# Half of the first layer's scales by TensorE, rotary tables moved ahead of the first products, normalization by k-tile

## The chip, the cores and the metric

The kernel runs on one core of a Trainium2 chip. The metric is device time in microseconds: the median of three runs of the program. Beside it stands one execution that was recorded by the hardware profiler; its span goes from the first to the last instruction.

## What is computed

Two layers of a decoder trunk on 256 tokens of 1024 channels, all in 32-bit floats. The part that the change touches is the start: the modulation of layer 0 from the conditioning vector `c`, and the first normalization.

```python
def rms_norm(x, g):
    xf = x.astype(jnp.float32)
    y = xf * lax.rsqrt(jnp.mean(xf * xf, axis=-1, keepdims=True) + NORM_EPS)
    return (y * g.astype(jnp.float32)).astype(x.dtype)
...
    cos_a, sin_a = rope_tables(positions, MLA_ROPE_DIM)
    cos_b, sin_b = rope_tables(positions, MOBA_HEAD_DIM)
    c_act = jax.nn.silu(c)
    for l in range(DEPTH):
        mod = c_act @ w_mod[l] + b_mod[l]
        sh1, sc1, g1, sh2, sc2, g2 = jnp.split(mod, 6, axis=-1)
        h = modulate(rms_norm(x, mix_norm_g[l]), sh1, sc1)
        y = token_mixer(h, cos_a, sin_a, cos_b, sin_b, w_in[l],
...
        x = x + g1[:, None, :] * y
        h = modulate(rms_norm(x, ffn_norm_g[l]), sh2, sc2)
        x = x + g2[:, None, :] * channel_mixer(h, w_up[l], ffn_dw_w[l], ffn_dw_b[l], w_down[l])
```

`modulate` is `h * (1 + scale) + shift`; `sh1` and `sc1` are parts r = 0 and r = 1 of `mod`, each a product of a 1024 vector with a 1024 x 1024 matrix.

## The kernel before, in words

Channels lie on the 128 partitions, in 8 k-tiles, and the 256 tokens along the free dimension. Each weight tile comes from memory as floats (`raw`, 512 KB for 1024 columns), ScalarE rounds it to `whi` (L211), VectorE takes the rest `wlo` (L213), and TensorE forms three products for each pair (L288, L289, L291). Activations are split likewise into `hh` (ScalarE, L765) and `hl` (VectorE, L766). SP issues all transfers; a semaphore of each of eight transfers is used again by the ninth after it, so an issue waits until the transfer eight places earlier has landed. Every engine works through its instructions in a fixed order, which a scheduler has set when the program was built: an instruction that waits holds all that stand behind it on its engine.

The start of layer 0 goes like this. SP loads the column of `c` (L341), x in four quarters (L343), then the first weight rows. ScalarE squares the eight k-tiles of x (L517), VectorE adds them up (L521), TensorE sums over channels with a column of ones (L525), VectorE scales (L469), GpSimd raises to the power of -1/2 (L470), TensorE spreads the result over the partitions (L499), ScalarE copies it out as `bcs` (L681), and VectorE multiplies all eight k-tiles of x by it (`xn`, in tile `mq`, L683).

The scales and shifts of layer 0 are made by VectorE: for each k-tile `prepare_tile(k)` loads one row tile of the transposed `w_mod` for the shift and one for the scale (`wload_row`, L687), multiplies each by the activated `c` and sums along the row (L692, 128 x 1024), adds the bias (L694) and makes the gain (L697). ScalarE applies gain and shift (L764), then L765 and L766 split the result, and `latents(k)` and `conv_in(k)` issue the first products of that k-tile. This loop over k runs at L758; `prepare_tile(k + 1)` stands between the two. Behind the loop stand the rotary tables: `make_trig` (some twenty VectorE instructions in a dependent chain, L416 to L438, and a sine by ScalarE, L439, which needs another function table), `make_bases` and `make_tables` (L449 to L461). After that come `GLU0` to `GLU3` (L830 with a Tanh, L831), which free the four PSUM banks of `conv_in`, and the first query, key and value products.

Other parts of `mod` are made by `mod_part`: TensorE multiplies the weight columns by `cact` as a stationary block of 32 columns at four column positions (L388), ScalarE copies the sum, TensorE transposes it and VectorE adds the bias.

PSUM has five banks of tag `psa` and three of `psb`.

Of the kernel before, what the change touches and what calls it, by code (L numbers as in the profile page):

```python
# [9 lines left out]
F32 = mybir.dt.float32  # L10
# [3 lines left out]
AF = mybir.ActivationFunctionType  # L14
# [3 lines left out]
P = 128  # L18
S = 256
NB = 2  # L20
D = 1024
# [127 lines left out]
def trunk_kernel(ctx, tc, xT, crow, ccol, pos, invf, modb_d, cols_d, grow_d, wmr, wm, win1, wqkv,  # L149
# [11 lines left out]
    def nm(s):  # L161
        uid[0] += 1
        return f"{s}_{uid[0]}"
# [10 lines left out]
    def mq(n=D):  # L174
        return wk.tile([P, D + 128], F32, tag="mq", name=nm("mq"), bufs=3, align_bytes=LINE)[:, 0:n]
# [11 lines left out]
    def small(n, tag="sm", bufs=12):  # L187
        return wk.tile([P, n], F32, tag=tag, name=nm(tag), bufs=bufs)
# [150 lines left out]
    x = per.tile([P, KD, S], F32, name="x")  # L339
    modb = per.tile([P, L, 48], F32, name="modb")  # L340
    sy.dma_start(cc, ccol)  # L341
    for i in range(4):
        sy.dma_start(x[:, 2 * i:2 * i + 2, :], xT[:, 2 * i:2 * i + 2, :])  # L343

    def load_rest():
        for dst, src in ((modb, modb_d), (posi, pos), (invt, invf)):
            sy.dma_start(dst, src)
        load_cols(0)
    col, grow = {}, {}

# [8 lines left out]
    def cv(l, name):  # L359
        a, b = COLS[name]  # L360
        return col[l][:, a:b]
# [4 lines left out]
    def wload_row(l, r, k, tag=None):  # L366
        return wload(wmr[ROWS.index((l, r)), k], tag or SPARE[(2 * k + r) % 4], 2 if tag else 1)
# [11 lines left out]
    def mod_part(l, r, spare=True):  # L379
# [15 lines left out]
        for q in range(2):  # L395
# [2 lines left out]
        ve.tensor_tensor(mod[l][:, r * 8:r * 8 + 8].rearrange("p (c q) -> p c q", c=4), view,  # L398
                         modb[:, l, r * 8:r * 8 + 8].rearrange("p (c q) -> p c q", c=4),
                         op=ALU.add)  # L400
        yield

    def mod_parts(*parts):
# [266 lines left out]
    def layer(l):  # L670
# [3 lines left out]
        hh, hl = new_h()  # L674
        if l == 0:

            bc = first_stats(crow0[1])
            xn = [mq().rearrange("p (k t) -> p k t", k=4) for _ in range(2)]

            bcs = e1()  # L680
            ac.activation(bcs, bc, AF.Copy)  # L681
            for k in range(KD):
                (gp if XNP and k else ve).tensor_tensor(xn[k // 4][:, k % 4, :], x[:, k, :], bcs, op=ALU.mult)  # L683
            mods0, gains = [], []

            def prepare_tile(k):
                raws0 = [wload_row(0, r, k) for r in range(2)]  # L687
                if k == 0:
                    load_rest()
                accs = small(2, "m0", 4)  # L690
                for r in range(2):
                    ve.scalar_tensor_tensor(raws0[r], raws0[r], 1.0, crow0[0], op0=ALU.mult, op1=ALU.mult,  # L692
                                            accum_out=accs[:, r:r + 1])
                mods0.append(ve.tensor_tensor(mod[0][:, 0:16].rearrange("p (r k) -> p k r", r=2)[:, k, :], accs,  # L694
                                              modb[:, 0, 0:16].rearrange("p (r k) -> p k r", r=2)[:, k, :], op=ALU.add))
                g = small(1, "gs", 12)
                i = ve.scalar_tensor_tensor(g, mod[0][:, 8 + k:9 + k], 1.0, cv(l, "mix_g")[:, k:k + 1],  # L697
                                            op0=ALU.add, op1=ALU.mult)
                gains.append(g)
                if HOLD:  # L700
                    hold[0] = i.ins

            prepare_tile(0)
        else:
            bc = norm_stats(fill)
# [52 lines left out]
        for k in range(KD):  # L758
# [10 lines left out]
            latents(k)  # L769
            if k + 1 < KD:  # L770
                prepare_tile(k + 1)
            else:
                with tc.issue_after(mods0[-1].ins):
                    make_trig()
            conv_in(k)
            if k in C0K:
                gate_c(0, C0K[k], 3, psa)
# [3 lines left out]
        mods = mod_parts(*((*p, False) for p in PARTS[l]))  # L781

        if l == 0:
            make_bases()
            with tc.issue_after(mods0[-1].ins):
                prepare(0)
        ta, tb, cw, gk, hg = prepared[l]


# [528 lines left out]
```

## Time and profile before

| what | us |
|---|---|
| median of 3 runs | 956.33 |
| the three runs | 953.44, 956.33, 961.74 |
| the profiled execution's own time | 960.24 |
| its span | 958.4 |
| TensorE busy | 910.8 |
| VectorE busy | 792.0 |
| ScalarE busy | 553.7 |
| GpSimd busy | 81.9 |

The span is what the rows below are measured in; the profiled execution's own time is 1.84 us longer than its span. Matmuls are pipelined, so busy time of TensorE is not time at its peak rate: the same product can take twice as long in another stretch.

### The profile page before, as it was taken

How to read it: one execution, taken by the hardware profiler on the slowest of the kernel's cores; microseconds unless marked ns; L12 is line 12 of the kernel's file. 1: busy time of each engine (PE TensorE's matmuls, PEld its weight loads, DVE VectorE, ACT ScalarE, POOL GpSimd, SP SyncE). 2: the span in 40 equal slices, each digit the busy share in tenths (PEclk: the TensorE clock that was granted, in tenths of full speed). 3: DMA queues.
4: the chain of work that ended last, by engine and by line, in shares of the span. 5: the costliest groups of instructions: out<-in, count | busy, mean ns of one | idle time of the engine just before them, and what ended most of it. 6: DMA issues, size and time to landing. Idle time of an engine off the chain costs nothing.

```text
span 958.4 us, 18539 instructions
## 1 busy us (share of the span) xinstructions
PE 910.8 (95%) x7262; PEld 852.6 (89%) x7262; DVE 792.0 (83%) x1524; ACT 553.7 (58%) x978; POOL 81.9 (9%) x48
## 2 busy tenths in 40 slices
PE   3999899799999999999899999979999999999998
PEld 2998788798997999999879987769999899999998
DVE  5999799799997899998874999967677798777774
ACT  4577488634655555555643675847565566555551
POOL 1011621300000000000000042231000000000000
PEclk9999999999998999999979999979999999999999
DMA  7966434388896878888753665505557767656641
GB/s 255 388 218 216 140 111 138 125 271 303 289 323 227 287 252 287 294 309 265 227 184 103 193 221 186 176 23 176 189 167 229 264 210 219 185 190 181 193 134 44
DMA packets 58120, 201.07 MB, mean 210 GB/s; under 512 B 6960, under 2 KB 8496, under 8 KB 58032
## 3 DMA queue, kind: packets, MB, share of 16 engines
q1 hardware_dynamic: 58032, 199.88, 62.4%
q8 instruction: 57, 0.93, 0.4%
q14 instruction: 31, 0.25, 0.1%
HBM read 198.81 MB, written 1.05 MB: 209 GB/s over the span
## 4 chain that ended last, share of the span: by engine, by line
PE 68%; DVE 11%; issue 8%; DMA 5%; POOL 4%; ACT 3%; SPq 0%; POOLq 0%; DVEq 0%; ACTq 0%
PE psb L288 13%; PE psb L291 13%; PE psb L289 13%; PE psa L288 6%; PE psa L289 6%; PE psa L291 6%; DVE wlo L213 3%; POOL rs L470 2%; DVE cacc L1015 2%; PE psa L388 2%; DMA raw<-in_wmr 2%; POOL ri L610 2%; ACT p L604 2%; DVE raw L371 1%; PE psa L628 1%
## 5 line engine op out<-in xcount | busy, mean ns | idle before, releaser
L211 ACT ACTIVATE whi<-raw 128x1024 fp32r<-128x1024 f32 (+2 forms) x286 | 294.4, 1037 | 217.0 <-PE psb L289 100.4
L213 DVE TENSOR_TENSOR wlo<-raw,whi 128x1024 fp32r<-128x1024 f32 (+2 forms) x286 | 340.4, 1194 | 82.6 <-ACT whi L211 71.4
L288 PE MATMUL psb<-hh,whi 128*128 128x256 f32 x1088 | 263.6, 283 | 1.2 <-ACT p L604 0.8
L289 PE MATMUL psb<-hl,whi 128*128 128x256 f32 x1088 | 260.8, 280 | 0.0
L288 PEld LDWEIGHTS psb<-hh,whi 128*128 128x128 f32 x1088 | 205.3, 189 | 9.1 <-issue 4.9
L289 PEld LDWEIGHTS psb<-hl,whi 128*128 128x128 f32 x1088 | 205.1, 189 | 1.4 <-DVE hl L534 1.1
L291 PE MATMUL psb<-hh,wlo 128*128 128x256 f32 x1088 | 150.5, 280 | 0.0
L291 PEld LDWEIGHTS psb<-hh,wlo 128*128 128x128 f32 x1088 | 136.8, 189 | 0.9 <-issue 0.8
L1015 DVE SCALAR_TENSOR_TENSOR cacc<-upad,cw,cacc 128x256 f32<-128x256 f32 x240 | 105.0, 480 | 0.4
L470 POOL TENSOR_TENSOR rs<-rs,mhalf 128x16 f32<-128x16 f32 (+3 forms) x22 | 48.8, 2228 | 585.6 <-DVE rs L469 581.5
L288 PE MATMUL psa<-mhl,whi 128*128 128x256 f32 x400 | 95.2, 279 | 0.0
L289 PE MATMUL psa<-mhl,whi 128*128 128x256 f32 x400 | 95.0, 279 | 0.0
L1194 DVE SCALAR_TENSOR_TENSOR e<-psb,fw,e 128x255 f32<-128x255 f32 (+1 forms) x176 | 83.9, 478 | 10.9 <-ACT e L1192 9.7
L288 PEld LDWEIGHTS psa<-mhl,whi 128*128 128x128 f32 x400 | 75.2, 189 | 0.2 <-ACT mhl L1096 0.2
L289 PEld LDWEIGHTS psa<-mhl,whi 128*128 128x128 f32 x400 | 75.2, 188 | 0.0
L1192 ACT ACTIVATE e<-psb,fb,fw 128x256 f32<-128x256 f32 x88 | 48.6, 553 | 34.9 <-DVE e L1194 21.1
L291 PE MATMUL psa<-mhl,wlo 128*128 128x256 f32 x400 | 54.6, 279 | 0.0
L371 DVE SCALAR_TENSOR_TENSOR raw<-raw,crow 128x1024 f32<-128x1024 f32 x40 | 48.7, 1218 | 2.9 <-DMA raw<-in_wmr 2.9
L291 PEld LDWEIGHTS psa<-mhl,wlo 128*128 128x128 f32 x400 | 50.1, 189 | 0.0
L610 POOL TENSOR_TENSOR ri<-smx,minus 128x4 f32<-128x4 f32 x16 | 31.5, 1978 | 93.2 <-ACT p L604 93.2
L288 PE MATMUL psb<-whi,hh 128*128 128x416 f32 (+1 forms) x96 | 32.0, 355 | 7.6 <-ACT hh L765 7.6
L388 PE MATMUL psa<-raw,cact 128*32 128x256 f32 x320 | 32.7, 445 | 0.4 <-DMA raw<-in_wm 0.4
(267 smaller groups left out, 1509.7 us busy)
## 6 DMA issues: line engine op xcount, KB each, us to landing
raw<-in_wup SPq DMA_DIRECT2D x88, 512.0 KB, 4.7
raw<-in_wmr SPq DMA_DIRECT2D x56, 512.0 KB, 5.2
raw<-in_wdn SPq DMA_DIRECT2D x44, 512.0 KB, 4.2
raw<-in_wm SPq DMA_DIRECT2D x40, 512.0 KB, 4.4
raw<-in_wgab SPq DMA_DIRECT2D x32, 512.0 KB, 4.7
raw<-in_wqkv SPq DMA_DIRECT2D x24, 512.0 KB, 4.8
raw<-in_win SPq DMA_DIRECT2D x16, 512.0 KB, 4.8
raw<-in_wgc SPq DMA_DIRECT2D x16, 512.0 KB, 4.2
```

The costliest lines, as they stand in the source:

```text
L211: ac.activation(hi, raw, AF.Copy)
L213: ve.tensor_tensor(lo, raw, hi.bitcast(F32), op=ALU.subtract)
L288: te.matmul(o, p1[0], p1[1], start=start, stop=False)
L289: te.matmul(o, p2[0], p2[1], start=False, stop=False)
L291: te.matmul(o, p3[0], p3[1], start=False, stop=stop)
L371: ve.scalar_tensor_tensor(raw, raw, scale, row, op0=ALU.mult, op1=ALU.mult, accum_out=acc)
L388: te.matmul(acc[32 * c:32 * c + 32, 0:S], cact[:, k:k + 1].to_broadcast([P, 32]), raw[:, c * S:(c + 1) * S], start=(k == 0), stop=(k == KD ...
L470: gp.tensor_tensor(r, r, mhalf[:, :n], op=ALU.pow)
L610: gp.tensor_tensor(ri, sm, minus1[:, 0:4], op=ALU.pow)
L1015: ve.scalar_tensor_tensor(aj, upad[:, j, t:t + S], cw[:, j * 31 + t:j * 31 + t + 1], aj, op0=ALU.mult, op1=ALU.add)
L1192: ac.activation(t, src, AF.Identity, scale=fw[:, 2, c:c + 1], bias=fb[:, c:c + 1])
L1194: ve.scalar_tensor_tensor(t[:, d:S], src[:, 0:S - d], fw[:, 2 - d, c:c + 1], t[:, d:S], op0=ALU.mult, op1=ALU.add)
```

## The change

- A new function `mod_first(0, 1)` makes half of layer 0's scales (r = 1, the channels of k-tiles 0 to 3) on TensorE. It loads the first 512 columns of the untransposed `w_mod` part, all eight k, as four transfers of 512 KB; multiplies them by `cact` in 32 products of 128 columns; copies the sum by ScalarE, transposes it by TensorE, adds the bias by VectorE. One `mod_gain` makes the four gains. `prepare_tile(k)` then has one row instead of two for k < 4.
- The positions and inverse frequencies are loaded before x. `load_rest` (bias, columns, rows of gains) is called behind the four new transfers.
- `make_trig` and `make_bases` are called behind `first_stats`, before the rest of `mod_first`, and no longer behind the loop; `prepare(0)` loses its place behind the last row.
- The multiplication of x by `bcs` moves into `prepare_tile(k)`, one k-tile at a time.

```diff
--- before.py
+++ after.py
@@ -339,12 +339,13 @@
     x = per.tile([P, KD, S], F32, name="x")
     modb = per.tile([P, L, 48], F32, name="modb")
     sy.dma_start(cc, ccol)
+    for dst, src in ((posi, pos), (invt, invf)):
+        sy.dma_start(dst, src)
     for i in range(4):
         sy.dma_start(x[:, 2 * i:2 * i + 2, :], xT[:, 2 * i:2 * i + 2, :])
 
     def load_rest():
-        for dst, src in ((modb, modb_d), (posi, pos), (invt, invf)):
-            sy.dma_start(dst, src)
+        sy.dma_start(modb, modb_d)
         load_cols(0)
     col, grow = {}, {}
 
@@ -398,6 +399,29 @@
         ve.tensor_tensor(mod[l][:, r * 8:r * 8 + 8].rearrange("p (c q) -> p c q", c=4), view,
                          modb[:, l, r * 8:r * 8 + 8].rearrange("p (c q) -> p c q", c=4),
                          op=ALU.add)
+        yield
+
+    def mod_first(l, r):
+
+        raws = []
+        for i, tag in enumerate(("qkT", "lh0", "qkT", "lh1")):
+            t = wk.tile([P, D], F32, tag=tag, name=nm("raw"), bufs=2 if tag == "qkT" else 1, align_bytes=LINE)
+            t = t.rearrange("p (k c) -> p k c", k=2)
+            sy.dma_start(t, wm[l, r, 2 * i:2 * i + 2, :, 0:D // 2].rearrange("k p c -> p k c"))
+            raws.append(t)
+        yield
+        acc = psa()
+        for k in range(KD):
+            for c in range(4):
+                te.matmul(acc[32 * c:32 * c + 32, 0:P], cact[:, k:k + 1].to_broadcast([P, 32]),
+                          raws[k // 2][:, k % 2, c * P:(c + 1) * P], start=(k == 0), stop=(k == KD - 1),
+                          tile_position=(0, 32 * c))
+        g = e1()
+        ac.activation(g[:, 0:P], acc[:, 0:P], AF.Copy)
+        pt = psa()
+        te.transpose(pt[:, 0:P], g[:, 0:P], ident)
+        ve.tensor_tensor(mod[l][:, r * 8:r * 8 + 4], pt[:, 0:P].rearrange("p (c m) -> p c m", c=4)[:, :, 0],
+                         modb[:, l, r * 8:r * 8 + 4], op=ALU.add)
         yield
 
     def mod_parts(*parts):
@@ -674,31 +698,36 @@
         hh, hl = new_h()
         if l == 0:
 
+
+            half = mod_first(0, 1)
+            step(half)
+            load_rest()
             bc = first_stats(crow0[1])
+            make_trig()
+            make_bases()
+            step(half)
             xn = [mq().rearrange("p (k t) -> p k t", k=4) for _ in range(2)]
 
             bcs = e1()
             ac.activation(bcs, bc, AF.Copy)
-            for k in range(KD):
-                (gp if XNP and k else ve).tensor_tensor(xn[k // 4][:, k % 4, :], x[:, k, :], bcs, op=ALU.mult)
-            mods0, gains = [], []
+            g4 = mod_gain(l, 1, "mix_g", 0, 4)
+            gains = [g4[:, k:k + 1] for k in range(4)]
 
             def prepare_tile(k):
-                raws0 = [wload_row(0, r, k) for r in range(2)]
-                if k == 0:
-                    load_rest()
+                n = 1 if k < 4 else 2
+                raws0 = [wload_row(0, r, k) for r in range(n)]
                 accs = small(2, "m0", 4)
-                for r in range(2):
+                for r in range(n):
                     ve.scalar_tensor_tensor(raws0[r], raws0[r], 1.0, crow0[0], op0=ALU.mult, op1=ALU.mult,
                                             accum_out=accs[:, r:r + 1])
-                mods0.append(ve.tensor_tensor(mod[0][:, 0:16].rearrange("p (r k) -> p k r", r=2)[:, k, :], accs,
-                                              modb[:, 0, 0:16].rearrange("p (r k) -> p k r", r=2)[:, k, :], op=ALU.add))
-                g = small(1, "gs", 12)
-                i = ve.scalar_tensor_tensor(g, mod[0][:, 8 + k:9 + k], 1.0, cv(l, "mix_g")[:, k:k + 1],
+                ve.tensor_tensor(mod[0][:, 0:16].rearrange("p (r k) -> p k r", r=2)[:, k, 0:n], accs[:, 0:n],
+                                 modb[:, 0, 0:16].rearrange("p (r k) -> p k r", r=2)[:, k, 0:n], op=ALU.add)
+                if k >= 4:
+                    g = small(1, "gs", 12)
+                    ve.scalar_tensor_tensor(g, mod[0][:, 8 + k:9 + k], 1.0, cv(l, "mix_g")[:, k:k + 1],
                                             op0=ALU.add, op1=ALU.mult)
-                gains.append(g)
-                if HOLD:
-                    hold[0] = i.ins
+                    gains.append(g)
+                ve.tensor_tensor(xn[k // 4][:, k % 4, :], x[:, k, :], bcs, op=ALU.mult)
 
             prepare_tile(0)
         else:
@@ -769,9 +798,6 @@
             latents(k)
             if k + 1 < KD:
                 prepare_tile(k + 1)
-            else:
-                with tc.issue_after(mods0[-1].ins):
-                    make_trig()
             conv_in(k)
             if k in C0K:
                 gate_c(0, C0K[k], 3, psa)
@@ -781,9 +807,7 @@
         mods = mod_parts(*((*p, False) for p in PARTS[l]))
 
         if l == 0:
-            make_bases()
-            with tc.issue_after(mods0[-1].ins):
-                prepare(0)
+            prepare(0)
         ta, tb, cw, gk, hg = prepared[l]
```

How the order of instructions moves, as the scheduler built it. First TensorE, from the sums of squares (`psb` <- `ones`) to the first products (`psb` <- `whi`). Before:

```order
L525 MATMUL psb_148<-ones,e_7_126 128x1 x2
L525 MATMUL psb_148<-ones,e_8_128 128x1 x2
L499 MATMUL psb_156<-ident,rs_153 128x128 x2
L288 MATMUL psb_196<-whi_201,hh_124 128x416
L288 MATMUL psb_198<-whi_201,hh_124 128x256
```

And now, where `psa` <- `raw,cact` are the new products and `psb` <- `ident,rs` is the spreading of the norm:

```order
L549 MATMUL psb_163<-ones,e_13_141 128x1 x2
L549 MATMUL psb_163<-ones,e_14_143 128x1 x2
L416 MATMUL psa_209<-raw_128,cact 32x128 x5
L523 MATMUL psb_171<-ident,rs_168 128x128 x2
L416 MATMUL psa_209<-raw_128,cact 32x128 x3
L416 MATMUL psa_209<-raw_130,cact 32x128 x8
L416 MATMUL psa_209<-raw_132,cact 32x128 x8
L416 MATMUL psa_209<-raw_134,cact 32x128 x8
L422 MATMUL psa_244<-ident,e_28_242 128x128
L288 MATMUL psb_267<-whi_272,hh_126 128x416
```

Five of the new products stand ahead of the spreading of the norm and 27 behind it, and all of them, with their transposition, ahead of the first product.

VectorE before, from the norm's scaling (`rs`) to the first gain (`gs`):

```order
L469 TENSOR_SCALAR rs_153<-psb_148 128x2
L692 SCALAR_TENSOR_TENSOR raw_171,m_25_182<-raw_171,crow_111 128x1024
L683 TENSOR_TENSOR mq_159<-x,e_20_161 128x256 x4
L683 TENSOR_TENSOR mq_160<-x,e_20_161 128x256 x4
L692 SCALAR_TENSOR_TENSOR raw_173,m_25_182<-raw_173,crow_111 128x1024
L213 TENSOR_TENSOR wlo_202<-raw_199,whi_201 128x672
L694 TENSOR_TENSOR mod_100<-m_25_182,modb 128x2
L213 TENSOR_TENSOR wlo_208<-raw_205,whi_207 128x1024
L697 SCALAR_TENSOR_TENSOR gs_186<-mod_100,col_178 128x1
```

Now the norm's scaling stands inside the chain that makes the angles (`e_24`, `e_25`, `e_26`): after the last sum of squares come fifteen instructions of that chain, then

```order
L493 TENSOR_SCALAR rs_168<-psb_163 128x2
```

then six more of the chain, eight copies of the sine table into `cs2a` and `cs2b`, and these:

```order
L678 TENSOR_SCALAR cw_766<-col_137 128x124
L485 TENSOR_TENSOR ta_756<-cs2a,grow_139 128x2x32
L423 TENSOR_TENSOR mod_102<-psa_244,modb 128x4
L730 TENSOR_TENSOR mq_247<-x,e_32_249 128x256
L564 SCALAR_TENSOR_TENSOR gs_251<-mod_102,col_137 128x4
L730 TENSOR_TENSOR mq_247<-x,e_32_249 128x256 x3
L721 SCALAR_TENSOR_TENSOR raw_253,m_35_255<-raw_253,crow_113 128x1024
L730 TENSOR_TENSOR mq_248<-x,e_32_249 128x256
L723 TENSOR_TENSOR mod_102<-m_35_255,modb 128x1
```

The angle chain has moved ahead of the normalization of x; between the first normalized tile and the shift that the first product needs stand fewer instructions than before.

ScalarE now, from the activated `c` (`crow`) to the first split activation (`hh`):

```order
L331 ACTIVATE crow_113<-psb_120 128x512
L463 ACT_TABLE_LOAD
L463 ACTIVATE trig<-e_24_175 128x192
L420 ACTIVATE e_28_242<-psa_209 128x128
L712 ACTIVATE e_32_249<-psb_171 128x256
L211 ACTIVATE whi_272<-raw_270 128x672
L793 ACTIVATE e_40_263<-mq_247,mod_102,gs_251 128x256
L794 ACTIVATE hh_126<-e_40_263 128x256
```

and at the end of the loop over k, where the Tanh of the first GLU needs its table back:

```order
L834 ACTIVATE b_150_807,lss_806<-ma_796 128x384
L854 ACT_TABLE_LOAD
L854 ACTIVATE e_141_784<-psa_259 128x256
```

Before, `bcs` (L681) followed `crow` directly, and no table load stood before the GLU. Now the sine and the copy of the new products' sum (L420) stand ahead of `bcs` (L712). The sine's table load stood behind the loop before, and the one that brought the other table back stood before the first exponentials of the attention; their number is three in both.

On SP the four new transfers stand behind x, and in place of the two first row tiles; the row tiles of the scales of k-tiles 0 to 3 are gone. So the same number of bytes is moved in the whole program, and 1 MB more ahead of the first weight tile.

## Rows read from the trace of the kernel before

**Rows 1.** Windows: length, busy PE, PEld, DVE, ACT, POOL, clock, DMA share, GB/s

```profile
0.00:22.88 22.88, 6.85 (x29) 6.20 (x29) 11.50 (x32) 9.12 (x19) 3.16 (x11) 1.00 0.75 247
28.00:62.68 34.68, 34.68 (x272) 34.42 (x271) 32.65 (x73) 20.28 (x37) 0.00 (x0) 1.00 0.88 336
```

**Rows 2.** The chain that ended last, 0 to 23 us: start, us, what

```profile
2.59 6.67 DMA x<-in_xT
...
12.36 1.64 POOL rs L470
...
15.30 0.39 ACT e L681
...
16.06 2.43 DVE mq L683 x7
18.49 1.14 DVE raw L692 x2
```

**Rows 3.** The same chain, 40 to 51 us: TensorE's last products of three k-tiles

```profile
40.76 0.61 PE psb L291 x4
...
45.35 0.61 PE psb L291 x4
...
50.38 0.61 PE psb L291 x4
```

**Rows 4.** Windows of the start (columns as in rows 1): while x arrives

```profile
1.18:5.79 4.61, 2.66 (x12) 2.69 (x13) 0.37 (x3) 1.77 (x4) 0.92 (x4) 1.00 0.62 179
5.79:9.28 3.49, 1.09 (x6) 0.80 (x4) 1.52 (x4) 1.45 (x4) 0.00 (x0) 1.00 0.97 343
3.50:5.00 1.50, 1.50 (x9) 1.50 (x9) 0.00 (x0) 0.40 (x2) 0.00 (x0) 1.00 0.84 212
```

**Rows 5.** Timeline of SP, 0 to 5 us: start, us, what it issues

```profile
1.18 1.84 SPq L343 DMA_DIRECT2D x<-in_xT  x4
```

**Rows 6.** Timeline of VectorE, 61 to 65 us: the angle chain behind the loop

```profile
61.55 0.25 DVE L427 TENSOR_SCALAR e<-e 128x192 f32<-128x192 f32 x1
61.83 0.26 DVE L428 TENSOR_SCALAR e<-e 128x192 f32<-128x192 f32 x1
...
64.22 0.35 DVE L436 SCALAR_TENSOR_TENSOR e<-e,e 128x192 f32<-128x192 f32 x1
```

**Rows 7.** Timeline of TensorE, three stretches: a product at either clock, and L388

```profile
27.03 0.41 PE L288 MATMUL psa<-hh,whi 128*128 128x256 f32 x1
28.51 0.28 PE L288 MATMUL psa<-hh,whi 128*128 128x256 f32 x1
290.99 1.07 PE L388 MATMUL psa<-raw,cact 128*32 128x256 f32 x16
297.05 2.78 PE L388 MATMUL psa<-raw,cact 128*32 128x256 f32 x22
```

**Rows 8.** Timelines of ScalarE and TensorE, 62 to 74 us

```profile
62.20 1.21 ACT L830 ACTIVATE e<-psa 128x256 f32<-128x256 f32 x4
...
72.29 1.28 ACT L439 ACT_TABLE_LOAD   x1
73.58 0.36 ACT L439 ACTIVATE trig<-e 128x192 f32<-128x192 f32 x1
...
63.14 0.45 PE L288 MATMUL psa<-whi,hh 128*128 128x512 f32 x1
```

**Rows 9.** What TensorE waited for, whole span: us in total, times, longest

```profile
PE psa L628 <- ACT p L619: 10.4, 3, 5.0
...
PE psa L568 <- ACT qkT L997: 3.1, 1, 3.1
...
PE psb L291 <- DVE wlo L213: 0.7, 1, 0.7
```

**Rows 10.** Timelines of VectorE and GpSimd, 170 to 178 us

```profile
170.68 6.42 DVE L1015 SCALAR_TENSOR_TENSOR cacc<-upad,cw,cacc 128x256 f32<-128x256 f32 x16
171.60 6.37 POOL L610 TENSOR_TENSOR ri<-smx,minus 128x4 f32<-128x4 f32 x1 [0.29 <-ACT p L604]
```

## The prediction

> **What bounds the kernel now.** I read the windows by stage first, then the chain of waits through the start, then the timelines around each edit. TensorE is busy in all of the 34.68 us from 28.00 to 62.68, and in only 6.85 of the first 22.88 us [rows 1]. So behind the start the kernel is bound by TensorE, and what the change can move is the moment of the first product, 22.88, and the few waits of TensorE later. The chain in front of that moment runs from the last quarter of x, which is issued at 2.59 and landed at 9.26, over the sums to GpSimd at 12.36, over the copy of the norm at 15.30 and eight multiplications of x to the second row multiplication at 18.49 [rows 2]. From the end of the copy, 15.69, to the first product it is 7.2 us. The reader should see that two things end late: x's last quarter, and VectorE's queue.
>
> **The change part by part.** All prices are from the one profiled execution, whose time is 960.24.
>
> *x later.* Positions and frequencies are two more issues ahead of x on SP; four issues of x take 1.84 us, so two take 0.9 [rows 5]. Behind x stand four transfers of scales where two row tiles stood. From 1.18 to 9.28 there moved 4.61 x 179 plus 3.49 x 343, that is 2.02 MB [rows 4]: when x's last quarter landed, nearly all of the two row tiles behind it had moved too. It shares the engines with its followers. The followers are now cut in rows of 2 KB, as x is, and not of 4 KB; while x moved alone the rate was 212 GB/s, later 343 [rows 4]. If the last 1.2 MB come at 212, they take 5.6 us and not 3.5. Bounds: +0.9 (only the issues) to +3.0; I take +2.0, the middle, since the rows show both the sharing and the slower rate but not their mixture.
>
> *The norm's scaling behind the angle chain.* VectorE ends the sums about 1.1 us after x has landed (ScalarE's and VectorE's last pair, each step near 0.4). Then the order puts fifteen instructions of the angle chain ahead of the scaling. Of these six are 192 wide and start 0.28 apart, four are of the 0.35 us kind, 0.27 to 0.38 apart by whether the next needs the result [rows 6], and five are shorter, near 0.15: together about 3.8 us. So GpSimd gets its operand 5.1 us after x has landed, against 12.36 - 9.26 = 3.1 now: +2.0. The sums on TensorE run beside this and do not add. Were x so late that part of the chain is done before, this falls towards 0.5; nothing in the order lets more than one of these instructions go ahead of the last sums.
>
> *The new products.* 27 of the 32 stand behind the spreading of the norm on TensorE. 22 records of L388, eleven products of 256 columns, took 2.78 us at the lower clock, 16 records 1.07 at the higher [rows 7]. 27 products of 128 columns are as many columns as 13.5 of those: 3.4 us at the lower clock, 1.8 at the higher. A product of 256 columns took 0.41 us at 27.03 and 0.28 at 28.51, so TensorE works at 1.2 GHz until about 28, after 7.6 us of waiting and 5.2 us of work [rows 7]; I take the lower clock, since here too it is mostly idle until GpSimd is done. ScalarE copies their sum ahead of the norm's copy (0.35 with the hand-over), and the transposition and bias add which stand ahead of the first multiplication of x cost another 0.35 beyond the norm's copy. Together 4.1, bounds 2.3 and 5.0.
>
> *From the norm to the first product.* Four multiplications of x at 2.43/7 = 0.35, the gain 0.1, one row multiplication 1.14 [rows 2], one more multiplication of x and the bias 0.15 make 3.15, and gain, shift and split on ScalarE another 1.1 as now. 4.3 in place of 7.2: -2.9. This is what the change gains at the start; the shift's row tile and the first weight tile have landed long before, at over 200 GB/s [rows 4] some 4 MB are in by 22 us.
>
> So the first product comes 2.0 + 2.0 + 4.1 - 2.9 = 5.2 us later, near 28.1.
>
> *The loop.* Four row multiplications go from VectorE (4 x 1.14). TensorE's last products of a k-tile stand 4.59 apart at 40.76 and 45.35 and 5.03 apart at 45.35 and 50.38 [rows 3], where VectorE's two rows end last. With VectorE ahead I expect 4.59 throughout: -0.4, bounds 0 and -1.2. If the loop began at the higher clock it would save half of the first 5.2 us, 2.6; I don't count it.
>
> *The table load.* The sine goes to the start, where ScalarE waits anyway. But the Tanh of the first GLU now needs its table back. It began at 62.20, VectorE's part behind it freed a bank, and TensorE's product for that bank followed at 63.14 [rows 8]. A load takes 1.28 [rows 8] and nothing else is queued on TensorE ahead of that product: +1.1, bounds 0 and 1.3. The GLUs behind it wait too, but only this one is waited for.
>
> In the Trainium skill, ScalarE: Activation LUTs, section What ACT_TABLE_LOAD costs, a switch is 1.28 us and a drain of 1.38 more, 2.66 in all. The trace agrees with the load alone: the load ends at 72.29 + 1.28 = 73.57 and the sine begins at 73.58, with no drain between [rows 8]. By the page the stall would be 2.5 and the whole sum 1.4 higher.
>
> *What goes behind the loop.* TensorE's wait of 0.7 for `wlo` [rows 9] lies behind the sine's load and the tables on VectorE: -0.7, bounds 0 and -1.3 (the exponentials' load too).
>
> Sum: 5.2 - 0.4 + 1.1 - 0.7 = +5.2, so 965.4 for an execution like the profiled one. That one is 3.9 above the median of the runs; against the median, 956.33 + 5.2 = 961.5. A difference under 1%, some 9.6 us, is about what a measurement of this kernel can't tell from no change.
>
> **The rivals.**
>
> *x starves.* The one that ends slower. If x's last quarter again lands only when all that stands behind it has moved, 3.07 MB and not 2.02, it comes at 5.79 + (3.07 - 0.83)/0.343 = 12.3 at the best rate and at 16.4 at 212 GB/s [rows 4], with the issues 4 to 8 later than now and not 2.0. For it: the 2.02 MB above. Against it: the issues are 0.46 apart [rows 5], so two of the four followers come in only when x has a lead. With 6.8 the sum is 10.0: 966.3. It decides from x landing 6.4 us later, near 15.7. The Trainium skill, DMA: Bandwidth & Descriptors, section Queues, rings and completion order, says that completion is not in the order of issue; the 6.67 us of x's last quarter [rows 2] agree, and by that page alone the quarter could wait for any of its followers.
>
> *A start at the higher clock.* TensorE has sums, five products, the spreading and 27 products in one stretch. If these bring it to 2.4 GHz, the 27 cost 1.6 less and the loop's first 5.2 us 2.6 less; with x at its lower bound (1.1 less) the sum is -0.1: 956.2. For it: some 5 us of work in a row. Against it: behind these products TensorE waits over 4 us for VectorE and ScalarE, and it came out of 7.6 us of waiting at the lower clock [rows 7].
>
> *VectorE's relief pays later.* The conv taps (L1015) move ahead of where they stood, since the tables are gone. TensorE waits 10.4 us for the scaled probabilities and 3.1 for `qkT` [rows 9]; if the longest, 5.0, and the 3.1 went, the sum is -2.9: 953.4. Against it: the 5.0 come from a GpSimd step of 6.37 us beside sixteen taps in a row [rows 10], and the order now has 22 there.
>
> **How the numbers follow.** Forecast 0.60, x starves 0.15, the higher clock 0.15, the relief 0.10. The three without starving leave almost all within 1%. Of the forecast some 0.07 lies above 1% (all upper bounds: 3.0 + 2.0 + 5.0 - 2.9 + 1.3 = 8.4, and runs scatter by 5), of the starving case 0.10, so slower is 0.17; faster 0.05, from the relief and the higher clock together (-8); same 0.78. The range goes from 952, below the relief's 953.4, to 968, above the starving case's 966.3.
>
> **What would show it.** Right: in the trace after, x's last quarter lands near 11, the norm's scaling stands inside the angle chain some 5 us behind it, the norm's copy waits for the copy of the products' sum, the first product comes near 28, and a wait of about 1 us for L855 stands at the end of the loop. Wrong: a first product before 22.88, a loop that begins with products of 0.28 us, or a landing of x behind 15. The forecast falls if the angle chain is over before x has landed, or if the 27 products are cheaper than 2 us.

## The result, and the profile after

| | before | after |
|---|---|---|
| median | 954.88 us, 4 runs | 970.04 us, 4 runs |
| span of the profiled execution | 958.4 us | 968.9 us |
| TensorE's wait for the scaled probabilities | 10.4 us [rows 9] | 19.2 us |

The ratio is 1.0117, with a 95% interval of 1.0072 to 1.0162: slower by 1.2%. The forecast was +5.2 us, within 1%, and 961.5; on its own base of 956.33 the ratio makes 967.5, near the range's upper end of 968, and the median itself, 970.04, lies above it. The spans differ by 10.5 us, twice the forecast, and the added time isn't where the forecast put it. Executions differ where the order is the same, too: the second layer's FFN, behind its norm's power, takes 197.7 and 197.8 us in the two traces of this section, but 190 to 192 in four of the nine other traces of whole kernels below, at a granted clock of 1.00 either way, so stages are compared below and not single spans. The start first. The chain that ended last, from the last quarter of x to the first product (start, us, what):

```profile
3.53 6.44 DMA x<-in_xT
...
15.14 0.08 DVE rs L493
...
15.30 0.81 POOL rs L494
...
16.16 1.22 PE psb L523 x4
17.38 3.17 PE psa L416 x54
...
20.64 0.29 ACT e L420
...
23.05 1.14 DVE raw L721 x2
...
24.70 0.61 ACT e L793
```

The chain comes in the order that was forecast: x, the angle chain up to the scaling at 15.14, the new products, the copy of their sum, the shift's row. The first product (L288) then starts at 25.80, 2.9 later than before [rows 1] and not 5.2. At the end of the loop the table load stands where it was expected. First the timeline of ScalarE there, then the one wait of TensorE from 62 to 100 us:

```profile
65.32 1.28 ACT L854 ACT_TABLE_LOAD   x1
66.61 1.21 ACT L854 ACTIVATE e<-psa 128x256 f32<-128x256 f32 x4
```

```profile
PE psa L288 <- DVE upad L855: 1.0, 1, 1.0
```

TensorE's product behind that wait starts at 67.50, before at 63.14 [rows 8]: the kernel is 4.4 behind. At the first reduction of the queries it is 0.6 behind (L897 at 108.96 before, L921 at 109.58 after). Between the two lie four powers on GpSimd for the norms ahead of the attention. GpSimd's timeline before (start and us first), and behind it the one after:

```profile
91.10 4.50 POOL L470 TENSOR_TENSOR rs<-rs,mhalf 128x16 f32<-128x16 f32 x2 [21.51 <-DVE rs L469]
96.00 9.44 POOL L470 TENSOR_TENSOR rs<-rs,mhalf 128x16 f32<-128x16 f32 x2 [0.40 <-DVE rs L469]
```

```profile
94.81 10.59 POOL L494 TENSOR_TENSOR rs<-rs,mhalf 128x16 f32<-128x16 f32 x4 [21.35 <-DVE rs L493]
```

They begin 3.7 later and end at the same time, 105.4: GpSimd took 13.9 us for them before and 10.6 after. So at 109 us the start has cost nearly nothing. The loss comes after that, in the attention. TensorE's longest waits in the whole span (us in total, times, longest us):

```profile
PE psa L652 <- ACT p L643: 19.2, 5, 6.8
PE psb L288 <- ACT hh L794: 4.4, 1, 4.4
```

Behind the wait for `p` stands GpSimd's reciprocal `ri` (a power of -1, L634), which ScalarE needs to scale the probabilities, and VectorE's conv taps beside it (a tap is one multiplication and addition of 128 x 256, for one position of the convolution). Timeline of VectorE, ScalarE, GpSimd and TensorE, 156 to 195 us:

```profile
156.57 6.02 DVE L1039 SCALAR_TENSOR_TENSOR cacc<-upad,cw,cacc 128x256 f32<-128x256 f32 x15
...
157.47 5.98 POOL L634 TENSOR_TENSOR ri<-smx,minus 128x4 f32<-128x4 f32 x1
...
176.66 8.80 DVE L1039 SCALAR_TENSOR_TENSOR cacc<-upad,cw,cacc 128x256 f32<-128x256 f32 x22
...
177.42 9.87 POOL L634 TENSOR_TENSOR ri<-smx,minus 128x4 f32<-128x4 f32 x2 [13.97 <-ACT p L628]
...
186.35 2.87 ACT L643 ACTIVATE p<-p,ri 128x128 f32<-128x128 f32 x8 [7.10 <-POOL ri L634]
...
186.81 0.47 PE L652 MATMUL psa<-ident,p 128*128 128x128 f32 x1 [6.84 <-ACT p L643]
...
186.94 0.56 PE L288 MATMUL psb<-hh,whi 128*128 128x256 f32 x1
...
194.39 0.28 PE L289 MATMUL psb<-hl,whi 128*128 128x256 f32 x1
```

A reciprocal that is begun 0.9 us into a run of taps ends 0.86 after the run has ended: 157.47 + 5.98 = 163.45 against 156.57 + 6.02 = 162.59. Before, the reciprocal beside sixteen taps did the same: it ended at 177.97, the taps at 177.10 [rows 10]. After the run of 22 taps TensorE has waited 6.84; its next product takes 0.56 and those behind it 0.41, as at 1.2 GHz in [rows 7], and they are back at 0.28 (2.4 GHz) at 194.39: the wait costs the clock too. Of the 19.2 us of waiting 6.8 stand behind the run of 22 and 4.5 behind the run of 15; in the same places before it was 5.0 and 0.6. Another 4.7, in the second layer, are there in both kernels, and 3.1 are new ahead of 150 us, behind the first two reciprocals of the attention (1.83 and 3.43 us, beside VectorE's rotary work and single taps). The windows of the kernel after (length, busy PE, PEld, DVE, ACT, POOL, granted clock, DMA share, GB/s) show it:

```profile
100.00:130.00 30.00, 26.90 (x158) 22.48 (x156) 26.01 (x51) 16.78 (x38) 17.62 (x6) 0.96 0.38 125
130.00:160.00 30.00, 29.19 (x236) 25.02 (x236) 26.95 (x57) 25.89 (x69) 6.00 (x4) 0.93 0.39 131
160.00:200.00 40.00, 29.08 (x234) 27.34 (x235) 24.87 (x52) 21.52 (x47) 13.32 (x3) 0.79 0.30 96
```

The last window in the kernel before:

```profile
160.00:200.00 40.00, 34.97 (x313) 32.55 (x313) 33.47 (x64) 21.99 (x45) 8.05 (x2) 0.96 0.47 156
```

TensorE is busy 29.08 of 40 us and not 34.97, at a clock of 0.79 and not 0.96. From 109.58 on the lag grows from 0.6 to 11.3 at the first gated output (L1075 at 191.61 before, L1099 at 202.88 after), and that is all of it: from the first FFN on the order of the instructions is the same.

### The profile page after: what moved, and what is told of

Its sections match the earlier page's. It is cut to its first block, busy times and chain, and to the rows that moved or that the text cites. A ratio compares the mean times of both kernels' runs of the same rounds, so it can differ in the third digit from the quotient of the medians.

```text
span 968.9 us, 18650 instructions
## 1 busy us (share of the span) xinstructions
PE 919.1 (95%) x7327; PEld 862.2 (89%) x7327; DVE 789.9 (82%) x1514; ACT 553.7 (57%) x979; POOL 83.4 (9%) x48
## 4 chain that ended last, share of the span: by engine, by line
PE 69%; DVE 9%; issue 8%; DMA 5%; POOL 4%; ACT 4%; SPq 0%; POOLq 0%; DVEq 0%; ACTq 0%
PE psb L288 13%; PE psb L291 13%; PE psb L289 13%; PE psa L288 7%; PE psa L291 7%; PE psa L289 7%; POOL ri L634 3%; DVE wlo L213 2%; DVE cacc L1039 2%; DMA raw<-in_wmr 2%; POOL rs L494 2%; PE psa L389 2%; ACT p L628 1%; PE psa L652 1%; PE psa L664 1%
## 5 line engine op out<-in xcount | busy, mean ns | idle before, releaser
L288 PE MATMUL psb<-hh,whi 128*128 128x256 f32 x1088 | 268.3, 286 | 1.0 <-ACT p L628 0.9
L289 PE MATMUL psb<-hl,whi 128*128 128x256 f32 x1088 | 265.4, 283 | 0.0
L288 PEld LDWEIGHTS psb<-hh,whi 128*128 128x128 f32 x1088 | 207.3, 191 | 8.5 <-issue 4.5
L289 PEld LDWEIGHTS psb<-hl,whi 128*128 128x128 f32 x1088 | 207.4, 191 | 1.1 <-DVE hl L558 0.8
L288 PE MATMUL psa<-mhl,whi 128*128 128x256 f32 x400 | 96.4, 281 | 0.2 <-ACT mhl L1120 0.2
L289 PE MATMUL psa<-mhl,whi 128*128 128x256 f32 x400 | 96.2, 281 | 0.0
L494 POOL TENSOR_TENSOR rs<-rs,mhalf 128x16 f32<-128x16 f32 (+3 forms) x22 | 42.2, 1923 | 593.7 <-DVE rs L493 592.9
L288 PEld LDWEIGHTS psa<-mhl,whi 128*128 128x128 f32 x400 | 75.4, 189 | 0.4 <-ACT mhl L1120 0.4
L634 POOL TENSOR_TENSOR ri<-smx,minus 128x4 f32<-128x4 f32 x16 | 39.7, 2487 | 94.0 <-ACT p L628 93.9
L652 PE MATMUL psa<-ident,p 128*128 128x128 f32 x96 | 21.1, 330 | 19.3 <-ACT p L643 19.2
L288 PE MATMUL psb<-whi,hh 128*128 128x416 f32 (+1 forms) x96 | 31.3, 353 | 4.5 <-ACT hh L794 4.4
```

The costliest lines, as they stand in the source:

```text
L288: te.matmul(o, p1[0], p1[1], start=start, stop=False)
L289: te.matmul(o, p2[0], p2[1], start=False, stop=False)
L494: gp.tensor_tensor(r, r, mhalf[:, :n], op=ALU.pow)
L634: gp.tensor_tensor(ri, sm, minus1[:, 0:4], op=ALU.pow)
L652: te.transpose(pp[:, n * P:(n + 1) * P], slots[n], ident)
```

## The experiments

My theory: the tables, moved to the start, make VectorE's order in layer 0's attention another one, with runs of 15 and 22 taps where 10, 4 and 16 stood; such a run holds GpSimd's reciprocal; TensorE waits. The rival: the start, with its later first product and its new products, is what costs. All ratios below are against the kernel before, run beside them.

**The tables back behind the loop.** All else of the change stays. (`mods0` collects the bias additions again, as before.)

```diff
             bc = first_stats(crow0[1])
-            make_trig()
-            make_bases()
             step(half)
...
+            else:
+                with tc.issue_after(mods0[-1].ins):
+                    make_trig()
             conv_in(k)
...
-            prepare(0)
+            make_bases()
+            with tc.issue_after(mods0[-1].ins):
+                prepare(0)
```

> All of the change except the place of the rotary tables: they stand behind the loop over k again, and the order of the attention of layer 0 is then that of the kernel before (10, 4 and 16 taps in a row between its steps, not 15 and 22). Theory (runs of conv taps hold up GpSimd's reciprocals, and TensorE waits for the scaled probabilities): that wait falls from 19.2 us to near 10.4, and the time is that of the kernel before to within 3 us, 952 to 958. Rival (the late first product, 25.8 instead of 22.9, and the new products are what costs): only the table load of 1.0 goes and the time stays at 965 to 969.

Measured: 955.51 us, ratio 1.0001 (0.9970 to 1.0032). TensorE's wait:

```profile
PE psa L652 <- ACT p L643: 11.3, 5, 5.0
```

As the theory has it: the wait is that of before within 0.9, and by its ratio the time can't be told from that of before. The first product came at 21.42 in this profile.

**The tables alone.** The kernel before with the early positions and `make_trig` and `make_bases` behind `first_stats`; nothing else of the change.

```diff
+    for dst, src in ((posi, pos), (invt, invf)):
+        sy.dma_start(dst, src)
     for i in range(4):
...
             bc = first_stats(crow0[1])
+            make_trig()
+            make_bases()
```

> The kernel before with one part of the change: positions loaded ahead of x and the rotary tables made at the start; no product for the scales on TensorE, all of x normalized at once. Its attention has the runs of 15 and 22 taps. Theory: TensorE waits near 19 us for the scaled probabilities and the time is 8 to 12 above before, 962 to 967. Rival (the start with its new products costs): 1 to 3 above before, 956 to 958.

Measured: 969.07 us, ratio 1.0111 (1.0045 to 1.0177), and

```profile
PE psa L629 <- ACT p L620: 19.8, 6, 6.8
```

This one part of the change gives its whole wait and, by the ratio, its whole loss; the time is above the expected 962 to 967. The trace shows that the loss lies in the attention: the first product comes late here too, at 25.88, but the power behind the first reduction of the queries starts at 110.43, level with the kernel before (110.73; 111.35 after all of the change). From there to the power of the conv's norm it is 137.7 us, against 130.1 before, 140.8 after all of the change and 132.7 in tables_back.

**Reciprocals on VectorE**, in both kernels: one constant, which takes the other branch at `ri`.

```diff
-RIP = 1
+RIP = 0
```

> The changed kernel with the reciprocal of the sums of the exponentials on VectorE, in its own queue, instead of GpSimd; the runs of taps are then cut in pieces of 3 to 14. Theory: the wait for the scaled probabilities falls from 19.2 to under 10 us and the time to 955 to 961. Rival (the start costs, GpSimd's delay is hidden anyway): within 2 us of the changed kernel, 967 to 970.

> The same edit in the kernel before. Theory: its wait of 10.4 us for the scaled probabilities, of which 5.0 beside sixteen taps in a row, falls to under 5 and the time by 4 to 8, to 947 to 951. Rival: no difference beyond 1 us.

Measured: the changed kernel 939.26 us, ratio 0.9820 (0.9766 to 0.9874); the kernel before 941.84 us, ratio 0.9861 (0.9815 to 0.9906). Both gain more than expected. In the changed kernel (first the waits, then the window and the timeline of VectorE):

```profile
PE psa L652 <- ACT p L643: 2.2, 1, 2.2
```

```profile
160.00:200.00 40.00, 38.64 (x355) 36.34 (x354) 38.87 (x74) 23.39 (x45) 0.00 (x0) 1.00 0.68 227
```

```profile
168.80 0.16 DVE L636 RECIPROCAL ri<-smx 128x4 f32<-128x4 f32 x1
168.89 2.04 DVE L1039 SCALAR_TENSOR_TENSOR cacc<-upad,cw,cacc 128x256 f32<-128x256 f32 x5
170.84 0.16 DVE L636 RECIPROCAL ri<-smx 128x4 f32<-128x4 f32 x1
```

The reciprocal is 0.16 us in VectorE's queue. The wait falls by 17.0. The time falls by more, from 1.0117 to 0.9820 of before, some 28 us; the clock of the window that had 0.79 is 1.00. By the two traces the stretch from the last norm ahead of the attention to the conv's norm is 17.3 us shorter in the first layer and 9.3 in the second. This version beats both kernels, the old one by 1.8%.

**What the parts of the change are worth then.** Three more kernels, all with reciprocals on VectorE: the tables behind the loop, no new products, and x normalized at once. The second and third edits:

```diff
-            half = mod_first(0, 1)
-            step(half)
...
-                n = 1 if k < 4 else 2
+                n = 2
```

```diff
+            for k in range(KD):
+                ve.tensor_tensor(xn[k // 4][:, k % 4, :], x[:, k, :], bcs, op=ALU.mult)
             g4 = mod_gain(l, 1, "mix_g", 0, 4)
...
-                ve.tensor_tensor(xn[k // 4][:, k % 4, :], x[:, k, :], bcs, op=ALU.mult)
```

> The kernel of tables_back (all of the change but the place of the tables) with the reciprocals on VectorE, so that no run of taps holds them up. Theory: what the change does at the start shows now by itself; the first product is at 21.4 instead of 25.8 and the load of 1.0 ahead of the GLU is gone, 3 to 5 below the changed kernel with reciprocals on VectorE (939.3): 934 to 937. Rival: the start is made up for by the loop and the attention in any case, 938 to 941.

> The changed kernel with reciprocals on VectorE and without the new products: all scales by VectorE again, two row tiles for each k-tile; tables at the start, x normalized k-tile by k-tile. Theory (the new products are worth it: 4 row multiplications of 1.14 off VectorE in the loop, against 3.2 us of products ahead of the first one): 2 to 5 above 939.3, 941 to 944. Rival (they cost as much as they give): 937 to 940.

> The changed kernel with reciprocals on VectorE and all eight multiplications of x ahead of the first row multiplication again. Theory: three multiplications of 0.35 more ahead of the first product, 1.0 later there: 939 to 942. Rival: as the changed kernel with reciprocals on VectorE within what can be told, 938 to 940.

| reciprocals on VectorE and | us | ratio | first product in the profile |
|---|---|---|---|
| the kernel before | 941.84 | 0.9861 (0.9815 to 0.9906) | 22.51 |
| all of the change | 939.26 | 0.9820 (0.9766 to 0.9874) | 25.76 |
| tables behind the loop | 940.71 | 0.9829 (0.9797 to 0.9860) | 24.29 |
| no new products | 942.51 | 0.9842 (0.9813 to 0.9871) | 19.95 |
| x at once | 941.91 | 0.9827 (0.9795 to 0.9858) | 27.46 |

The intervals overlap; none of the parts can be told from no difference. So the times of the last two, within their theories' 941 to 944 and 939 to 942, confirm neither theory: "no new products" is 2.2 thousandths above "all of the change", less than either interval's half-width of 2.9 and 5.4. 7.5 us between the earliest and the latest first product don't show in the time. For the tables the theory's 934 to 937 was a miss: the first product was not at 21.4 this time, though the start is the same program as in tables_back. x's last quarter landed at 8.80 there (3.53 + 5.27) and some 2 us later here, where ScalarE's last two squares begin at 10.70.

**How a run holds GpSimd.** Here the theory became narrower, and one part of it fell. The first probe begins three powers beside runs of one kind:

> The disputed cost by itself: nothing of the trunk is computed; three dependent powers of 128 x 4 on GpSimd, the reciprocal's form, are begun together with a run on VectorE, once beside nothing and then beside 24 instructions of one kind, 128 x 256: conv taps (two operands in SBUF), taps into changing tiles, taps with one operand in PSUM, additions of two operands, multiplications of one operand, copies, taps with a short one-operand instruction behind every fourth, and last 12 taps. Theory: the first power takes 0.7 beside nothing and lasts until the run ends (some 9.6 us for 24 taps, 4.8 for 12) beside taps; short pieces let it in. Rival (GpSimd is only slowed, or it is the dependence of one tap on the last): the first power takes 1 to 3 us beside all kinds, or is held beside dependent taps alone.

Timelines of VectorE and GpSimd, the run of 24 taps:

```profile
9.36 12.46 DVE L333 SCALAR_TENSOR_TENSOR o<-x,w,o 128x256 f32<-128x256 f32 x24
...
9.49 1.23 POOL L372 TENSOR_TENSOR ri<-smx,minus 128x4 f32<-128x4 f32 x1 [1.14 <-DVE smx L358]
```

1.23 us, against 1.02 beside nothing: nothing is held, and in none of the other kinds either (1.01 to 1.23). So a run of taps as such doesn't hold the power. In the kernel the taps of two channel groups alternate, which leaves no gap between them (8.80/22 = 0.40 us each); in the probe each tap waits for the one before (12.46/24 = 0.52). Two runs followed from this. One has the kernel's alternating taps:

> Nothing of the trunk is computed. The first probe's powers began with the first instruction of the run and its taps either waited on the one before or wrote tiles that nothing read; in the kernel the taps of two channel groups alternate, each waits for the last but one, and the power begins later, behind ScalarE. Here: 24 taps alternating over two accumulators, with the power released by 1 to 8 copies on ScalarE, so 0.3 to 2 us into the run; then taps in one chain, over four accumulators, alternating taps with a short instruction behind every fourth, alternating additions, alternating one-operand multiplications, and no run at all. Theory: beside taps without a gap between them a power begun inside the run stays until the run's end (6 to 9 us), beside taps in one chain, whose spacing of 0.52 us leaves a gap of 0.04 between them, it takes 1.0 to 1.3. Rival (the kernel's powers wait for something else that ends with the run): 1.0 to 1.3 in all of them.

```profile
23.12 9.58 DVE L338 SCALAR_TENSOR_TENSOR cacc<-upad,cw,cacc 128x256 f32<-128x256 f32 x24
...
24.06 1.19 POOL L377 TENSOR_TENSOR ri<-s,minus 128x4 f32<-128x4 f32 x1 [7.79 <-DVE cacc L338]
...
164.86 6.38 DVE L338 TENSOR_SCALAR cacc<-cacc,cw 128x256 f32<-128x256 f32 x24
...
165.50 5.78 POOL L377 TENSOR_TENSOR ri<-s,minus 128x4 f32<-128x4 f32 x1 [5.07 <-DVE cacc L338]
```

At all eight delays the first power takes 1.0 to 1.3 beside alternating taps. The one kind that holds it, twice in two, is a multiplication of one operand, alternating between two tiles: 165.50 + 5.78 = 171.28, the end of the run. The other run puts the taps of the changed kernel in one chain, with GpSimd's reciprocals left as they were:

```diff
             for t in range(t0, t1):
+                with ExitStack() as es:
+                  if tapped:
+                    es.enter_context(tc.issue_after(tapped[-1].ins))
...
+                tapped.append(i)
```

> The changed kernel, reciprocals on GpSimd as there, but VectorE takes the conv taps strictly one channel group after the other, so that each tap depends on the one just before it; runs of 8, 9, 13 and 15 such taps stand beside the reciprocals. Theory (what holds GpSimd is taps without a gap, not taps): no reciprocal takes over 2 us, the wait for the scaled probabilities falls from 19.2 to under 8 us, and the time falls to 945 to 960, some of the gain lost to taps of 0.52 instead of 0.40 (124 a layer, 15 us of VectorE) and to their other places. Rival (any run of taps holds GpSimd until its end): reciprocals of 4 to 7 us and a time within 5 us of the changed kernel's.

Measured: 963.55 us, ratio 1.0052 (1.0022 to 1.0082). The waits, and the timelines of VectorE and GpSimd:

```profile
PE psb L1057 <- DVE e L1056: 12.7, 1, 12.7
PE psa L652 <- ACT p L643: 5.2, 1, 5.2
```

```profile
157.08 4.64 DVE L1043 SCALAR_TENSOR_TENSOR cacc<-upad,cw,cacc 128x256 f32<-128x256 f32 x9
...
157.03 2.10 POOL L634 TENSOR_TENSOR ri<-smx,minus 128x4 f32<-128x4 f32 x2 [8.66 <-ACT p L628]
```

Beside these runs no reciprocal takes over 1.7, and the wait falls from 19.2 to 5.2. What is left of it has another cause. It stands behind a reciprocal that took 4.03, the first of the two in this row (the timelines of GpSimd and VectorE again):

```profile
125.70 5.63 POOL L634 TENSOR_TENSOR ri<-smx,minus 128x4 f32<-128x4 f32 x2 [5.11 <-ACT p L628]
...
126.38 2.49 DVE L938 TENSOR_TENSOR mq<-mq,tb 128x512 f32<-128x512 f32 x4
```

It ended at 129.73, 0.86 behind the four rotary multiplications, which have two operands and leave no gap (0.60 apart, 0.68 each). In the changed kernel a reciprocal of 3.43 ended 0.87 behind the same four. So it doesn't take taps. The time is above the expected 945 to 960; the taps in one chain make the conv late, with 12.7 us of a new wait. So the edit, which also moved the taps, shows that taps without a gap hold the reciprocal in the kernel, and the trace that other work without a gap does too; but alternating taps alone, in the probe, don't. Two guesses at what else it takes were tried. In the changed kernel the small tiles were moved, with the same order on every engine:

```diff
+    low = ctx.enter_context(tc.tile_pool(name="low", bufs=1))
...
-        return wk.tile(
+        return (low if tag in ("smx", "ri") else wk).tile(
```

> The changed kernel, every engine's order the same row for row; only the eight tiles of 16 bytes a partition that the reciprocal reads and writes lie elsewhere (from 227392 on, before 209120 and 215392, close behind the taps' accumulators at 204768). Theory A (a reciprocal and a tap meet at addresses, and the reciprocal loses each time): no reciprocal is held beside the runs of 15, 22 and 18 taps, the wait for the scaled probabilities falls under 6 us, and the time to 944 to 952. Theory B (it is taps without a gap, wherever the operands lie): the same three are held for 6 to 9 us until the run ends, and the time stays at 966 to 971.

Measured: 969.02 us, ratio 1.0108 (1.0070 to 1.0146), and

```profile
PE psa L653 <- ACT p L644: 19.8, 5, 6.8
```

The same three are held. The last run is a probe with the changed kernel's addresses, with and without transfers of weights (349 GB/s in its first half, 91 over its second):

> Nothing of the trunk is computed. As in the second probe, 22 alternating taps with a power released by 2 to 6 copies on ScalarE, now with all tiles at the addresses that they have in the changed kernel, the first thirteen stretches beside weight tiles of 512 KB that stream in, the last thirteen without; in the last three of each thirteen, one-operand multiplications instead of taps. If addresses cause the holding, powers of 5 to 9 us appear in both halves; if it needs transfers beside the taps, in the first half alone; if neither, all powers beside taps take 1.0 to 1.4 and what holds them in the kernel stays open. Beside one-operand multiplications the power lasts until the run ends, as it did in the second probe (5.78 and 4.95).

```profile
93.91 7.96 DVE L352 TENSOR_SCALAR cacc<-cacc,cw 128x256 f32<-128x256 f32 x30
...
94.62 7.29 POOL L381 TENSOR_TENSOR ri<-smx,minus 128x4 f32<-128x4 f32 x1 [5.65 <-ACT smx L376]
```

All twenty first powers beside taps took 1.0 to 1.4, in both halves; all six beside one-operand multiplications lasted until the run's end (6.8 to 7.3). So neither these addresses nor transfers are by themselves the second condition.

## Why the prediction was right and wrong

The direction was right, and +5.2 was half of what came. That the time still lies in the forecast's range is luck: the range's upper end was set by x starving and by upper bounds at the start, and neither came. By its own steps:

- *x later*, +2.0: +0.7 (landed at 9.97, before at 9.26 [rows 2]), below the lower bound of 0.9. The four followers did not take x's share, and *x starves* fell. The two landings above, of one program, are 2 us apart: the term is as large as its scatter. The 6.67 us of x's last quarter, which the prediction took to agree with landings out of order, show none: before, the quarter landed at 9.26, and the issues that wait for the two row tiles behind it went out at 10.57 and 11.81.
- *The norm's scaling behind the angle chain*, 5.1 after x: 15.14 - 9.97 = 5.2. Right, and the power got its operand 2.2 later. Not foreseen: the power took 0.81 instead of 1.64 [rows 2].
- *The new products*, 3.4 us at the lower clock: 3.17 (54 records, two for each product). From the power's end to the norm's copy it was 1.30 before [rows 2] and 4.7 now (16.11 to 20.81, where L712 begins): +3.4. The transposition and the bias add came on top: x's first multiplication (L730, 21.64) starts 0.45 behind the norm's copy, and before it was 0.03. That makes +3.8, forecast +4.1.
- *From the norm to the first product*, 4.3: 25.80 - 21.64 = 4.2, against 22.88 - 15.72 = 7.2 before: -3.0, forecast -2.9. Right. Sum of the start: 0.7 + 2.2 - 0.8 + 3.8 - 3.0 = 2.9, forecast 5.2; the difference is mostly x and the power.
- *The loop*, -0.4: +0.3 (25.80 to 65.90, against 22.88 to 62.68). The row tiles off VectorE gave nothing that shows, and the *start at the higher clock* did not come: products of 0.41 and more until about 32 us.
- *The table load*, +1.1: 1.0. Right. The drain of 1.38 that the Trainium skill has beside the load (ScalarE: Activation LUTs, section What ACT_TABLE_LOAD costs) isn't there this time either: the load ends at 66.60, the Tanh begins at 66.61, and the instruction ahead of the load ends at 65.29, 0.03 before it. *Behind the loop*, -0.7: the wait for `wlo` is gone, and four powers gave back some 3 us more. They take 9.5 to 10.6 in all nine kernels that have some part of the change, tables_back among them, and 13.9 in the two that have none; which edit does it isn't known.
- *The rival of VectorE's relief* saw the right place. Its mechanism was that taps move forward and shorten the waits for `p`; against it the prediction held the 6.37 us beside sixteen taps in a row [rows 10] and the 22 taps in the new order. It used that row only to doubt a gain, and gave it no price. This is the step that failed: the sum had no term for the attention, where the wait grew by 8.8 us. The same row would have given one: a reciprocal that lasts as long as its taps costs 2.4 us more with 22 of 0.40 us than with 16, and a second run of 15 costs nearly the 5.0 that 16 did [rows 9]. That makes 7, with both landing as the row has it. Measured, the wait behind the longer run grew by 1.8, the one behind the run of 15 by 3.9, and 3.1 came behind the attention's first two reciprocals, which stand in none of the rows.

That the tables' place makes the order, and the order the wait and the loss, is shown by two runs that undo it and do it alone. That the wait hangs on GpSimd's reciprocals is shown by the runs without them, which also cut the runs of taps into pieces. That four faster powers repaid the start is read from the traces and wasn't tried by itself.

## What to carry to other kernels

Where a scheduler fills an engine's gaps, a change at the start moves the fill everywhere behind it: read the order beside every long wait of the old profile, and price what stands there now. A short operation on the path belongs on an engine whose queue is in order and near: 0.16 us behind a few taps beat 1 to 9 us on an engine of its own. And a first product that comes some microseconds earlier is worth nothing if what follows has slack of that size.

## What the runs showed of the hardware

A power on GpSimd lasted until VectorE's run had ended in two kinds of places: beside one-operand multiplications that alternate between two tiles in the probes, eight times of eight (5.0 to 7.3 us), and beside work of two operands without a gap in the kernels, alternating taps or rotary multiplications, there not always. Of the other kinds in the first probe neither one-operand multiplications in a chain (0.39 us each) nor copies without a gap (0.21 each) held it: the power took 1.09 and 1.18. In the kernel before it was so in the second layer, in the middle of eighteen taps; the reciprocal that began with the same run was not held:

```profile
628.10 7.21 DVE L1015 SCALAR_TENSOR_TENSOR cacc<-upad,cw,cacc 128x256 f32<-128x256 f32 x18
...
628.17 1.27 POOL L610 TENSOR_TENSOR ri<-smx,minus 128x4 f32<-128x4 f32 x1 [14.74 <-ACT p L604]
630.15 6.03 POOL L610 TENSOR_TENSOR ri<-smx,minus 128x4 f32<-128x4 f32 x1 [0.70 <-ACT p L604]
```

What decides it beside taps stays open: not the form of the taps alone, not the addresses that were tried, not transfers. In the kernels the held reciprocals above ended 0.86 to 0.87 after the run, nearly the whole of an undisturbed one (1.01); in the probes with one-operand multiplications within 0.06. So they may be two mechanisms; that wasn't tried.

The Trainium skill, SBUF — State Buffer, section Who interferes with whom, says that an instruction of VectorE in a two-port mode takes a pair of ports that it shares with GpSimd for the whole instruction, that the second to come is blocked, and that an instruction with two inputs in SBUF contends with a GpSimd instruction that reads SBUF. Among the kinds that can enter such a mode it has copies and multiplications of one operand. The probes agree on the alternating one-operand multiplications, and go further: the power was blocked for 19 to 28 instructions and not for one. On the copies (1.18) they don't agree. On two operands they differ: beside taps the first power took 1.0 to 1.4 us, against 1.01, while one tap lasts 0.48. By that page alone every tap run would hold every reciprocal, or none for longer than a tap; neither is what the kernels show.
